# A two-layer transformer trunk in one kernel: in its linear attention, the 64-row products of the two halves of the array are issued alternately, into two PSUM banks

## The chip, the cores and the metric

The kernel runs on one core of a Trainium2 chip. The metric is device time in microseconds (us) of one execution. A profile is one further execution recorded by the hardware; its engines are PE (TensorE, the 128x128 matrix array), PEld (loads of the stationary operand into that array), DVE (VectorE), ACT (ScalarE) and SP (which issues the DMAs). GpSimd does no work here.

## The reference, cut to what matters

Two layers work on 256 latent and 256 context tokens of width 1024. Each layer projects its normalised input, feeds three token mixers (latent attention, bidirectional gated linear attention, neighbourhood attention), merges their outputs by gates, and adds a feed-forward block. Only the linear attention is touched by the change. It has 4 heads with 64-wide keys and 128-wide values, and works in chunks of 64 tokens, once forwards and once backwards:

```python
def gla_chunked(q, k, v, log_a, s0):
    ...
    cum = jnp.cumsum(log_a, axis=3)
    last = cum[:, :, :, -1:, :]
    q_dec = q * jnp.exp(cum)
    k_inv = k * jnp.exp(-cum)
    k_end = k * jnp.exp(last - cum)
    ...
    att = jnp.where(lower, jnp.einsum('bhncd,bhnsd->bhncs', q_dec, k_inv), 0.0)
    o_intra = jnp.einsum('bhncs,bhnse->bhnce', att, v)
    kv_chunk = jnp.einsum('bhncd,bhnce->bhnde', k_end, v)
    decay = jnp.exp(last[:, :, :, 0, :])
    def step(state, inp):
        dec, kv = inp
        return dec[..., None] * state + kv, state
    ...
    o_inter = jnp.einsum('bhncd,bhnde->bhnce', q_dec, s_prev)
    return (o_intra + o_inter).reshape(b, h, l, dv), s_final
```

Two of these products matter below: `kv_chunk` (sum over the 64 tokens of a chunk) and the scores `att` (sum over the 64 key channels). Both sum over 64, half of the array's 128 rows.

## The kernel before

Nothing in the kernel is issued directly. The code records every operation into a plan (`_Plan.record`), with the operations that it depends on and a price in ns (`price`). When all is recorded, `schedule` lays the operations out on a modelled clock: each engine takes the ready operation with the earliest due time, the due times follow from the prices and the recorded order of the PE operations, and a buffer is taken only when one is free. There are 8 PSUM banks of 512 fp32 columns (tag `b`), 70 general SBUF slabs (`s`), and three buffers each for raw, high and low weight tiles. `emit` then writes the instructions out in the order found; every instruction has the line of that call, L486, in the profile, so groups are told apart by tile names. On the chip each engine runs its own list in that order and waits on semaphores.

The recorded order comes from `drive`: it takes the main matrix work (`mains`, generators that yield the price of what they recorded) and, in proportion to the work done, pulls steps from a `filler` generator, up to `ftotal` in all. In the stage that matters the filler is `gla()`, the linear attention; the mains are the projections of its values (`tm` with `ev_v`, PSUM tile `zt`) and gates (`ev_g`), then `merge(1, yC)`, which alternates gate projections (`fm`, PSUM tile `z`) and output projections of the neighbourhood attention (`proj`). After it comes `merge(2, yB)`, which needs the result of the linear attention. The values that the filler yields set how fast it advances beside the mains. Weights come by DMA into `raw`, ACT rounds them to `hi`, DVE forms the rest `lo`, and three passes (hi, lo) make one product; these passes are of type float32r. The products of the linear attention are in plain float32, and each shows as two passes (two MATMUL records) in the profile.

`gla()` for one layer:

- `gla_prep`: cumulated decays by products of 64 output columns (PSUM tile `gc`), alternating between the two column halves of the array; then exponentials.
- `kv(t)`, for a tile of 128 tokens (two chunks): four transposes into `gkt`, copied by ACT into `gkT`; then for each of the two chunks (`half`) four products of 64 rows, one for each head, into a bank `gkv` of its own; DVE scales each by the decay into `gkvs` (`tensor_scalar`, four per chunk).
- `att(t)`: for each direction `d` four score products of 64 rows into a bank `gat`; DVE writes them under a mask into `attz` (`copy_predicated`), then adds both directions into `gatt`.
- `scan`: the states `gS`, by `scalar_tensor_tensor` on DVE, forwards in the upper and backwards in the lower partitions.
- `o_tile(t)`: for each head one product of 128 rows (`go<-tv,gatt`) and two of 64 output columns (`go<-gS,gqk`), for the two chunks, into the two column halves; then squares on ACT (`gjk`), a reciprocal root by small DVE steps (`grv`, `gry`, `gra`, `grb`), `gyt`, transposes `gyT`, and the split result `ybh`, `ybl`.

The first layer has 4 calls of `kv` and 4 of `att`; the second, whose context output isn't needed, 4 of `kv` and 2 of `att`. That is 14 calls, 28 runs of four products with 64 rows, 112 products, 224 passes.

The price of such a product is that of a full one, `max(4 * n / 2.4, 1.67 * m) + 5.4`, 219 for 128 columns. `record` makes one exception (L252 to L261): a float32 product with at most 64 output columns that follows one in another column half is priced at 56 (27 for 32 columns).

Of the kernel before, what the change touches and what calls it, by code (L numbers as in the profile page):

```python
# [9 lines left out]
F32 = mybir.dt.float32  # L10
# [4 lines left out]
ALU = mybir.AluOpType  # L15
# [129 lines left out]
def _meets(a, b):  # L145
    if a[1] <= b[0] or b[1] <= a[0] or a[3] <= b[2] or b[3] <= a[2]:
        return False
    if a[4] is None and b[4] is None:
        return True
    sa = a[4] if a[4] is not None else range(a[2], a[3])  # L150
    sb = b[4] if b[4] is not None else range(b[2], b[3])
    if a[4] is None:
        return any(x in sa for x in sb)
    return any(x in sb for x in sa) if b[4] is None else not sa.isdisjoint(sb)
# [27 lines left out]
class _Plan:  # L182
# [15 lines left out]
    def record(self, eng, name, args, kw):  # L198
        op = _Op()
        op.eng, op.name, op.args, op.kw, op.idx = eng, name, args, kw, len(self.ops)  # L200
        op.func = args[2] if name == "activation" else None
        w, r = [], []
        if "out" in kw:
            w.append(kw["out"])
            rest = list(args)
        else:
            w.append(args[0])
            rest = list(args[1:])
        for k, v in kw.items():
            if k == "accum_out":  # L210
                w.append(v)
            elif k != "out":
                rest.append(v)
        r = [v for v in rest if isinstance(v, _View)]
        w = [v for v in w if isinstance(v, _View)]
        if name == "copy_predicated" or (name == "matmul" and not kw.get("start", True)):
            r.append(w[0])
        deps = set()
        op.bufs = []
        op.allocs = []  # L220
        for v in r:
            g = v.region()
            deps.update(o for o, q in v.buf.writes if _meets(g, q))
        for v in w:
            g = v.region()
            if v.buf.space == "psum" and eng == "pe":
                prev = [o for o, q in v.buf.writes]
                deps.update(prev[-1:])
                deps.update(o for o, q in v.buf.reads)
            else:  # L230
                deps.update(o for o, q in v.buf.writes if _meets(g, q))
                deps.update(o for o, q in v.buf.reads if _meets(g, q))
        for v in r:
            v.buf.reads.append((op.idx, v.region()))
        for v in w:
            g = v.region()
            if v.buf.first is None:
                v.buf.first = op.idx
                op.allocs.append(v.buf)
            v.buf.writes = [x for x in v.buf.writes if not (g[4] is None and x[1][0] >= g[0] and x[1][1] <= g[1] and x[1][2] >= g[2] and x[1][3] <= g[3])]  # L240
            v.buf.reads = [x for x in v.buf.reads if not (g[4] is None and x[0] != op.idx and x[1][0] >= g[0] and x[1][1] <= g[1] and x[1][2] >= g[2] and x[1][3] <= g[3])]
            v.buf.writes.append((op.idx, g))
        for b in {id(v.buf): v.buf for v in r + w}.values():
            op.bufs.append(b)
            b.left += 1
        deps.discard(op.idx)
        op.deps = deps
        op.pin = self.last_pe if self.pinned else None
        op.cost, op.bytes = self.price(eng, name, w, r, kw)
        if eng == "pe":  # L250
            self.last_pe = op.idx
            rows = w[0].p1 - w[0].p0  # L252
            if name == "matmul" and r[0].dtype == F32 and rows <= 64:
                if self.lead and w[0].p0 not in self.lead:
                    op.cost = 56.0 if rows > 32 else 27.0
                    self.lead.add(w[0].p0)
                else:
                    self.lead = {w[0].p0}
            else:
                self.lead = set()  # L260
        self.ops.append(op)  # L261
        return op
# [227 lines left out]
def tile_trunk(ctx: ExitStack, tc: tile.TileContext, xin, wst, wm0, wmt, cbc_in, ct_in, cols_in, fin_in,  # L490
               glan_in, gw_in, nab_in, const_in, out):
    nc = _Plan(CAPS, HORIZON)

    def const_tile(shape, dt, tag, name):
        return nc.tile(tag, shape, dt, name)

    def slab(name, dt=F32, shape=None):
        return nc.tile("s", shape or [128, 512], dt, name)
# [7 lines left out]
    def bank(name, shape=None):  # L506
        return nc.tile("b", shape or [128, 512], F32, name, "psum")

    if True:
# [43 lines left out]
        gmask = (const[:, 1024:1536].bitcast(U32), const[:, 1536:2048].bitcast(U32))  # L553
        ct = const_tile([128, 8, 2], F32, "ct", "ct")
        h = []
        for k in range(KD):
            t = slab(f"x{k}")
# [3 lines left out]
        for l in range(L):  # L561
            t = const_tile([128, 69], F32, f"cols{l}", f"cols{l}")
# [365 lines left out]
        for l in range(L):  # L928
# [10 lines left out]
                                           op0=ALU.mult, op1=ALU.add)  # L939
# [206 lines left out]
            gv = [None] * 4  # L1146
            gs = [None] * 4
            qq, kk = [None] * 4, [None] * 4
# [54 lines left out]
            dec = const_tile([128, 4, 8], F32, "dec", f"dec{l}")  # L1203
# [97 lines left out]
            def gla():  # L1301
# [10 lines left out]
                bufs = []  # L1312
                for d in range(2):
                    t = slab(f"attz{d}")
# [4 lines left out]
                def kv(t):  # L1319
                    ps = bank("gkt", [128, 4, 128])  # L1320
                    for hh in range(4):
                        nc.tensor.transpose(ps[:, hh], kk[hh][:, 128 * t : 128 * t + 128], ident)
                    kt = slab("gkT")
                    nc.scalar.copy(kt, ps)
                    yield 430
                    for half in range(2):
                        r = slice(64 * half, 64 * half + 64)
                        c = 2 * t + half
                        pk = bank("gkv", [128, 4, 128])
                        for hh in range(4):  # L1330
                            nc.tensor.matmul(pk[:, hh], kt[r, 128 * hh : 128 * hh + 128], gv[t][r, 128 * hh : 128 * hh + 128], start=True, stop=True)
                        s = slab("gkvs", shape=[128, 4, 128])
                        for hh in range(4):
                            nc.vector.tensor_scalar(out=s[:, hh], in0=pk[:, hh], scalar1=dec[:, hh, c : c + 1], scalar2=None, op0=ALU.mult)
                        kvs[c] = s
                        yield 860

                def att(t):
                    w = slice(128 * t, 128 * t + 128)
                    a = slab("gatt")  # L1340
                    for d in range(2):
                        r = slice(64 * d, 64 * d + 64)
                        ps = bank("gat", [128, 4, 128])
                        for hh in range(4):
                            nc.tensor.matmul(ps[:, hh], kk[hh][r, w], qq[hh][r, w], start=True, stop=True)
                        nc.vector.copy_predicated(bufs[d], gmask[d], ps.rearrange("p a b -> p (a b)"))
                        yield 860
                    nc.vector.tensor_tensor(out=a, in0=bufs[0], in1=bufs[1], op=ALU.add)
                    atts[t] = a

# [44 lines left out]
                for cf in ([4, 5, 6, 7], [0, 1, 2, 3]):  # L1395
                    tt = (cf[0] // 2, cf[0] // 2 + 1)
                    for t in tt:
                        yield from kv(t)
                        if t in ts:
                            yield from att(t)  # L1400
                    st = scan(cf, cf[::-1], Sp, st)
                    for t in tt:
                        if t in ts:
                            o_tile(t)
                            yield 2600
                    for c in cf[1:3]:
                        del kvs[c]
                    atts.clear()
                for hh in range(4):
                    ps = bank("gyT", [128, 4, 128])  # L1410
# [20 lines left out]
            if not last:  # L1431
                h = []
                for k in range(KD):
                    t = slab(f"h{k}")
# [138 lines left out]
        for i in range(2):  # L1573
            t = slab(f"fdiag{i}")
# [5 lines left out]
        for k in range(KD):  # L1580
            c = slice(128 * (k % 4), 128 * (k % 4) + 128)
            for j in range(2):
                nc.tensor.matmul(po[j][k // 4][:, c], h[k][:, 128 * j : 128 * j + 128], fdiag[k // 4][:, c], start=True, stop=True)
        for j in range(2):
            for i in range(2):
                t = slab(f"o{j}_{i}")
# [7 lines left out]
    ps = ctx.enter_context(tc.tile_pool(name="ps", bufs=1, space=bass.MemoryType.PSUM))  # L1594
# [117 lines left out]
```

## Time and profile before

| | us |
|---|---|
| median of 3 runs | 1548.5 (1545.71 to 1548.73) |
| the profiled execution | 1543.93 |
| its span, first to last instruction | 1542.1 |
| DVE busy | 1089.3 (71%) |
| ACT busy | 763.3 (49%) |
| linear attention of layer 1, first `gkv` pass to last `gat` pass | 372.8 to 453.3 |
| the same of layer 2 | 1219.0 to 1261.9 |

The granted TensorE clock is 0.996 of full speed on average. The timeline of PE has a row for each run of equal instructions: start, length from the first start to the last end, the operation with the rows and columns of the array that it uses (64*128 is 64 rows by 128 columns), and the size of the moving operand. Passes are pipelined, so rows overlap: a pass of 256 columns lasts 0.28 us in its record but starts about 0.118 us after the one ahead of it. Costs are read from start to start.

### The profile page before, as it was taken

The page shows a single profiled execution, that of the slowest core. Times are in us where ns is not written, and L with a number is a line of the kernel's source. Part 1 is how long each engine was busy: PE and PEld are TensorE (multiplying, and loading weights), DVE is VectorE, ACT ScalarE, POOL GpSimd, SP SyncE. Part 2 cuts the span into 40 slices and gives each one's busy share as a digit, 9 for nine tenths or more (in the row PEclk, how much of TensorE's full clock was granted, in tenths as well). Part 3 has the DMA queues.
Part 4 walks back from the last instruction along what each step waited for, and adds up shares of the span by engine and source line. Part 5 has one row for each costly group of instructions (what it writes and reads, how often), then busy time and mean ns, then how long its engine had stood idle before and what let it go on. Part 6 is the DMA issues. An engine that isn't in the chain of part 4 may idle for free.

```text
span 1542.1 us, 24547 instructions
## 1 busy us (share of the span) xinstructions
PE 1523.3 (99%) x9566; PEld 1311.6 (85%) x9566; DVE 1089.3 (71%) x2174; ACT 763.3 (49%) x1363; POOL 0.2 (0%) x4
## 2 busy tenths in 40 slices
PE   8999999999999999999999999999999999999998
PEld 4687787789877899888888889887998999999998
DVE  5799989989888789633333336898476797776565
ACT  4669745576223345332232234679567535564443
POOL 0000000000000000000000000000000000000000
PEclk9999999999999999999999999999999999999999
DMA  9442244533335775622223224432342234455553
GB/s 365 148 157 99 101 157 168 172 131 123 103 110 174 248 268 179 204 93 91 92 90 100 96 91 143 143 113 82 105 145 87 99 107 164 164 195 190 178 190 112
DMA packets 67157, 222.68 MB, mean 144 GB/s; under 512 B 7964, under 2 KB 8348, under 8 KB 67040
## 3 DMA queue, kind: packets, MB, share of 16 engines
q1 hardware_dynamic: 67040, 221.11, 42.1%
q8 instruction: 75, 1.23, 0.3%
q14 instruction: 42, 0.34, 0.1%
HBM read 220.03 MB, written 1.05 MB: 143 GB/s over the span
## 4 chain that ended last, share of the span: by engine, by line
PE 94%; ACT 3%; DVE 2%; issue 0%; DMA 0%; SPq 0%; DVEq 0%
PE z L486 22%; PE fg L486 12%; PE fu L486 12%; PE fo L486 12%; PE zt L486 8%; PE proj L486 7%; PE wo L486 4%; PE zf L486 2%; PE mas L486 1%; PE nao L486 1%; PE nas L486 1%; PE mat L486 1%; PE go L486 1%; PE nat L486 1%; PE mao L486 1%; PE gkv L486 1%
## 5 line engine op out<-in xcount | busy, mean ns | idle before, releaser
L486 ACT CAST hi<-raw 128x1024 fp32r<-128x1024 f32 (+3 forms) x305 | 313.5, 1028 | 507.4 <-PE z L486 115.4
L486 DVE TENSOR_TENSOR lo<-raw,hi 128x1024 fp32r<-128x1024 f32 (+3 forms) x305 | 364.5, 1196 | 170.3 <-ACT hi L486 167.2
L486 PE MATMUL z<-uh,hi 128*128 128x512 f32 (+2 forms) x632 | 227.2, 360 | 0.0
L486 PE MATMUL z<-uh,lo 128*128 128x512 f32 (+2 forms) x632 | 219.8, 348 | 0.7 <-DVE lo L486 0.7
L486 PE MATMUL z<-ul,hi 128*128 128x512 f32 (+2 forms) x632 | 220.3, 349 | 0.0
L486 DVE SCALAR_TENSOR_TENSOR junk<-wm,cbc 128x1024 bf16<-128x1024 f32 x132 | 160.7, 1217 | 7.8 <-DMA wm<-in_wmt 6.8
L486 PEld LDWEIGHTS z<-uh,hi 128*128 128x128 f32 (+1 forms) x632 | 118.3, 187 | 23.6 <-issue 7.5
L486 PEld LDWEIGHTS z<-uh,lo 128*128 128x128 f32 (+1 forms) x632 | 118.1, 187 | 18.1 <-DVE lo L486 0.9
L486 PEld LDWEIGHTS z<-ul,hi 128*128 128x128 f32 (+1 forms) x632 | 118.4, 187 | 15.8 <-issue 0.7
L486 PE MATMUL fo<-hh,lo 128*128 128x256 f32 (+1 forms) x408 | 127.5, 314 | 0.0
L486 PE MATMUL fo<-hl,hi 128*128 128x256 f32 (+1 forms) x408 | 127.4, 314 | 0.0
L486 PE MATMUL fo<-hh,hi 128*128 128x256 f32 (+1 forms) x408 | 127.2, 314 | 0.0
L486 PE MATMUL fg<-uf,lo 128*128 128x256 f32 (+1 forms) x344 | 115.1, 335 | 0.0
L486 PE MATMUL fg<-ug,hi 128*128 128x256 f32 (+1 forms) x344 | 114.8, 334 | 0.0
L486 PE MATMUL fg<-uf,hi 128*128 128x256 f32 (+1 forms) x344 | 114.8, 334 | 0.0
L486 PE MATMUL fu<-uf,lo 128*128 128x256 f32 (+1 forms) x336 | 113.6, 338 | 0.0
L486 PE MATMUL fu<-uf,hi 128*128 128x256 f32 (+1 forms) x336 | 113.6, 338 | 0.0
L486 PE MATMUL fu<-ug,hi 128*128 128x256 f32 (+1 forms) x336 | 113.4, 338 | 0.0
L486 PE MATMUL zt<-hi,uh 128*128 128x256 f32 x352 | 102.4, 291 | 0.0
L486 PE MATMUL zt<-hi,ul 128*128 128x256 f32 x352 | 99.5, 283 | 0.0
L486 PE MATMUL zt<-lo,uh 128*128 128x256 f32 x352 | 99.1, 282 | 0.0
L486 PEld LDWEIGHTS fo<-hh,lo 128*128 128x128 f32 x408 | 76.5, 188 | 5.4
(402 smaller groups left out, 3204.8 us busy)
## 6 DMA issues: line engine op xcount, KB each, us to landing
raw<-in_wst SPq DMA_DIRECT2D x257, 512.0 KB, 3.5
wm<-in_wmt SPq DMA_DIRECT2D x82, 512.0 KB, 3.9
raw<-in_wst SPq DMA_DIRECT2D x40, 448.0 KB, 3.2
wmr<-in_wm SPq DMA_DIRECT2D x9, 512.0 KB, 7.2
nab<-in_nab SPq DMA_DIRECT2D x16, 256.0 KB, 3.8
fr<-in_wst SPq DMA_DIRECT2D x10, 256.0 KB, 5.8
raw<-in_wst SPq DMA_DIRECT2D x6, 384.0 KB, 3.0
x<-in_xin SPq DMA_DIRECT2D x8, 256.0 KB, 5.1
```

Source lines behind the costliest of these rows:

```text
L486: getattr(eng[o.eng], o.name)(*[real(a) for a in o.args], **{k: real(v) for k, v in o.kw.items()})
```

## The change

The two runs of four products in `kv(t)`, and in `att(t)`, are merged into one run of eight: two banks are taken at once, and for each head the product of the upper 64 rows is followed by that of the lower 64 rows. The DVE operations behind them are the same and in the same recorded order. The two yields of 860 become one of 1200. In `record`, the exception for the price is widened: it holds for a product with at most 64 rows too, where row half and column half together differ from those of the run so far.

```diff
             rows = w[0].p1 - w[0].p0
-            if name == "matmul" and r[0].dtype == F32 and rows <= 64:
-                if self.lead and w[0].p0 not in self.lead:
+            deep = r[0].p1 - r[0].p0
+            if name == "matmul" and r[0].dtype == F32 and min(rows, deep) <= 64:
+                at = (r[0].p0, w[0].p0)
+                if self.lead and at not in self.lead:
                     op.cost = 56.0 if rows > 32 else 27.0
-                    self.lead.add(w[0].p0)
+                    self.lead.add(at)
                 else:
-                    self.lead = {w[0].p0}
+                    self.lead = {at}
...
                     yield 430
+                    pk = [bank("gkv", [128, 4, 128]) for _ in range(2)]
+                    for hh in range(4):
+                        for half in range(2):
+                            r = slice(64 * half, 64 * half + 64)
+                            nc.tensor.matmul(pk[half][:, hh], kt[r, 128 * hh : 128 * hh + 128], gv[t][r, 128 * hh : 128 * hh + 128], start=True, stop=True)
                     for half in range(2):
-                        r = slice(64 * half, 64 * half + 64)
                         c = 2 * t + half
-                        pk = bank("gkv", [128, 4, 128])
-                        for hh in range(4):
-                            nc.tensor.matmul(pk[:, hh], kt[r, 128 * hh : 128 * hh + 128], gv[t][r, 128 * hh : 128 * hh + 128], start=True, stop=True)
                         s = slab("gkvs", shape=[128, 4, 128])
                         for hh in range(4):
-                            nc.vector.tensor_scalar(out=s[:, hh], in0=pk[:, hh], scalar1=dec[:, hh, c : c + 1], scalar2=None, op0=ALU.mult)
+                            nc.vector.tensor_scalar(out=s[:, hh], in0=pk[half][:, hh], scalar1=dec[:, hh, c : c + 1], scalar2=None, op0=ALU.mult)
                         kvs[c] = s
-                        yield 860
+                    yield 1200
...
                     a = slab("gatt")
+                    pa = [bank("gat", [128, 4, 128]) for _ in range(2)]
+                    for hh in range(4):
+                        for d in range(2):
+                            r = slice(64 * d, 64 * d + 64)
+                            nc.tensor.matmul(pa[d][:, hh], kk[hh][r, w], qq[hh][r, w], start=True, stop=True)
                     for d in range(2):
-                        r = slice(64 * d, 64 * d + 64)
-                        ps = bank("gat", [128, 4, 128])
-                        for hh in range(4):
-                            nc.tensor.matmul(ps[:, hh], kk[hh][r, w], qq[hh][r, w], start=True, stop=True)
-                        nc.vector.copy_predicated(bufs[d], gmask[d], ps.rearrange("p a b -> p (a b)"))
-                        yield 860
+                        nc.vector.copy_predicated(bufs[d], gmask[d], pa[d].rearrange("p a b -> p (a b)"))
+                    yield 1200
```

Since prices and yields set the order of the whole plan, the lists of the engines move too. Two places on PE follow; a row is one kind of product with its count.

The first is in layer 1, at the score products of one token tile. Before, the two runs of four stand with six passes of a gate projection (`z`) between them:

```order
L486 MATMUL proj<-ych,lo_4440 128x512
L486 MATMUL gat<-gqk 128x128 x4
L486 MATMUL z<-uh_0_266,hi_4443 128x512
L486 MATMUL z<-ul_0_310,hi_4443 128x512
L486 MATMUL z<-uh_0_266,lo_4458 128x512
L486 MATMUL z<-uh_1_317,hi_4443 128x512
L486 MATMUL z<-ul_1_361,hi_4443 128x512
L486 MATMUL z<-uh_1_317,lo_4458 128x512
L486 MATMUL gat<-gqk 128x128 x4
```

In the changed kernel the score products of such a tile stand between passes of a gate projection as one run:

```order
L488 MATMUL z<-ul_1_361,hi_4308 128x512
L488 MATMUL z<-uh_1_317,lo_4336 128x512
L488 MATMUL gat<-gqk 128x128 x8
L488 MATMUL z<-uh_2_383,hi_4308 128x512
L488 MATMUL z<-ul_2_392,hi_4308 128x512
```

The eight products are now one run. So it is at all 14 places: PE's list had 28 runs of four products with 64 rows, each between full products, and has 14 runs of eight.

The second place is in layer 2, at `o_tile` of the second token tile. Before, its twelve products stand together, four times one full product and the pair of the two column halves:

```order
L486 MATMUL go<-tv,gatt 128x128
L486 MATMUL go<-gS_12243,gqk 64x128
L486 MATMUL go<-gS_12190,gqk 64x128
L486 MATMUL go<-tv,gatt 128x128
L486 MATMUL go<-gS_12243,gqk 64x128
L486 MATMUL go<-gS_12190,gqk 64x128
```

In the changed kernel the beginning of the same tile reads so:

```order
L488 MATMUL go<-tv,gatt 128x128
L488 MATMUL proj<-ycl,hi_12222 128x256
L488 MATMUL go<-gS_12133,gqk 64x128
L488 MATMUL proj<-ych,lo_12297 128x256
L488 MATMUL z<-uh_0_8736,hi_12248 128x256
L488 MATMUL z<-ul_0_8909,hi_12248 128x256
L488 MATMUL proj<-ych,hi_12222 128x256
L488 MATMUL go<-gS_12061,gqk 64x128
L488 MATMUL go<-tv,gatt 128x128
L488 MATMUL go<-gS_12133,gqk 64x128
L488 MATMUL go<-gS_12061,gqk 64x128
L488 MATMUL go<-tv,gatt 128x128
```

The first pair of halves is torn apart by full products, the second still stands together. Over both tiles of layer 2 the 16 half products stood in 8 pairs, and now stand in 3 pairs and 10 single ones. In layer 1 they stay in 16 pairs.

## The prediction

> **What bounds the kernel now.** I read the page first: busy times, then the chain that ended last, then who PE waited for.
>
> ```profile
> span 1542.1 us, 24547 instructions
> PE 1523.3 (99%) x9566; PEld 1311.6 (85%) x9566; DVE 1089.3 (71%) x2174; ACT 763.3 (49%) x1363; POOL 0.2 (0%) x4
> PE 94%; ACT 3%; DVE 2%; issue 0%; DMA 0%; SPq 0%; DVEq 0%
> PE mat L486 <- DVE map L486: 3.9, 2, 2.0
> PE n0p L486 <- DVE sq L486: 1.9, 1, 1.9
> ```
>
> PE is busy for 99% of the span, and the chain that ended last runs through PE for 94% of it. The list of PE's waits begins with 3.9 us and 1.9 us, and none of its ten entries names a tile of the linear attention. So time taken out of PE's list there is time off the end, as long as nothing else comes late. A busy PE doesn't say what a product costs, though, since records overlap; that I read from start to start in PE's timeline around one run of the products.
>
> ```profile
> 372.23 0.28 PE L486 MATMUL zt<-hi,ul 128*128 128x256 f32 x1
> 372.35 0.28 PE L486 MATMUL zt<-hi,uh 128*128 128x256 f32 x1
> 372.47 0.28 PE L486 MATMUL zt<-lo,uh 128*128 128x256 f32 x1
> 372.58 0.28 PE L486 MATMUL zt<-hi,ul 128*128 128x256 f32 x1
> 372.79 1.16 PE L486 MATMUL gkv<-tv,gkT 64*128 64x128 f32 x8
> 373.88 0.39 PE L486 MATMUL zt<-hi,uh 128*128 128x256 f32 x1
> 374.10 0.28 PE L486 MATMUL zt<-lo,uh 128*128 128x256 f32 x1
> ...
> 379.38 0.28 PE L486 MATMUL zt<-hi,ul 128*128 128x256 f32 x1
> 379.59 1.16 PE L486 MATMUL gat<-gqk 64*128 64x128 f32 x8
> 380.68 0.38 PE L486 MATMUL zt<-hi,uh 128*128 128x256 f32 x1
> 380.90 0.28 PE L486 MATMUL zt<-lo,uh 128*128 128x256 f32 x1
> ```
>
> Full passes of 256 columns start every 0.118 us (372.23 to 372.58 is three of them). From 372.58 to 374.10 are 1.52 us, and two such passes lie in it, 0.24; the run of four products (8 passes) therefore costs PE **1.28 us**. The run of `gat` gives the same: 380.90 - 379.38 - 0.24 = 1.28.
>
> How that splits is in the durations of the passes, which the view of one tile lists as minimum, median and maximum.
>
> ```profile
> L486 PEld LDWEIGHTS gkv<-tv,gkT x128: 182/188/188, 372.8 to 1254.7; 64*128 64x128 f32 x128
> L486 PE MATMUL gkv<-tv,gkT x128: 272/272/374, 372.8 to 1254.8; 64*128 64x128 f32 x128
> ```
>
> The first pass of a run lasts 374 ns, the others 272: the extra 102 ns is its operand load, which nothing covers. Take 0.374 from the run's 1.16 and seven starts remain, 0.112 us a pass. So 8 x 0.112 = 0.90 is streaming, and 1.28 - 0.90 = **0.38 us is paid on entering and leaving** the 64-row form, whatever stands in the run. The next full pass (0.39 long, the one behind it 0.22 later) shows the same on the way out.
>
> **The change, part by part.** *Runs merged.* 28 runs become 14, so the 0.38 is paid 14 times less. That part is sure if the order is as built: 14 x 0.38 = 5.3 us.
>
> *Halves alternated.* No row of this trace has two row halves in turn, so the price of that is bounded by its nearest relatives. If the halves only take turns, a merged run has 16 passes of 0.112 plus 0.38, 2.17 us. If they stream side by side, two passes share a slot: 8 x 0.112 + 0.38 = 1.28, what a run of half the products costs now. The relative is the decay product `gc`, which alternates between two column halves:
>
> ```profile
> 358.36 0.28 PE L486 MATMUL zt<-hi,ul 128*128 128x256 f32 x1
> 358.57 1.09 PE L486 MATMUL gc<-const,gla 128*64 128x128 f32 x16
> 359.60 0.39 PE L486 MATMUL zt<-hi,uh 128*128 128x256 f32 x1
> 359.82 0.28 PE L486 MATMUL zt<-lo,uh 128*128 128x256 f32 x1
> ...
> L486 PEld LDWEIGHTS gc<-const,gla x128: 132/137/137, 345.9 to 1212.4; 128*64 128x64 f32 x128
> L486 PE MATMUL gc<-const,gla x128: 272/273/323, 345.9 to 1212.5; 128*64 128x128 f32 x128
> ```
>
> Its 16 passes cost 359.82 - 358.36 - 0.24 = 1.22 us: two by two they take (1.09 - 0.323) / 7 = 0.110 a slot, and the first pass shows an uncovered load of 51 ns for 64 columns, where `gkv` shows 102 for 128. Put the larger load in and the relative says 1.22 + 0.05 = 1.27, against 1.28 by the other way. I take 1.28, since it is the relative with alternation that the merged run is nearest to. Each merged run then saves 2 x 1.28 - 1.28 = 1.28, and 14 of them **17.9 us**; the other end, 2.17, leaves 14 x 0.39, about 5.4. Below 1.28 nothing is to be had, because a slot is one stream of 128 columns at 0.110 in either form.
>
> Here the Trainium skill speaks against the change. "TensorE: Matmul & The Clock Gate", section "LDWEIGHTS (loading the stationary operand)", says that a load's time goes with the columns alone, so that a load of few rows takes as long as a full one: 128 columns would be an estimated 107 ns, close to the 102 above. If the two halves' loads, 128 columns each here, then queue one behind the other, the slot of two passes is set by two loads, and the sum ends at the 5.4. "TensorEngine Tiling (Array Packing)", "Key Properties", says instead that tiles load and multiply in parallel and that only a change of mode drains the array, not a change of tile; by it the sum ends at 17.9. No run here shows row halves; the column halves agree with the second.
>
> *Pairs torn apart.* In layer 2 the order has 13 visits to the 64-column form for `go` where 8 were. What a pair and what a single one cost stands side by side once, at `gc`:
>
> ```profile
> 1198.17 0.38 PE L486 MATMUL zt<-hi,ul 128*128 128x256 f32 x1
> ...
> 1198.72 0.44 PE L486 MATMUL gc<-const,gla 128*64 128x128 f32 x4
> 1199.09 0.39 PE L486 MATMUL zt<-hi,ul 128*128 128x256 f32 x1
> 1199.41 0.43 PE L486 MATMUL gc<-const,gla 128*64 128x128 f32 x2
> 1199.77 0.39 PE L486 MATMUL zt<-hi,uh 128*128 128x256 f32 x1
> ```
>
> 1198.17 to 1199.09 is three full passes (0.35) and a pair: 0.57. 1199.09 to 1199.77 is one full pass (0.12) and a single product: 0.56. A half product alone costs as much as two, so each of the 5 visits more adds 0.56: **+2.8 us**. This one is given back whatever the rows do.
>
> *What is late next.* PE's list from the first `gkv` to the first product with `ybh` holds the same work in both kernels. In layer 2 it took 1219 to 1286; there PE becomes 6 x 1.28 - 2.8 = 4.9 us quicker, and DVE, which makes all that lies between, must follow.
>
> ```profile
> 1219.00:1287.00 68.00, 68.00 (x539) 62.72 (x539) 60.71 (x164) 26.76 (x52) 0.00 (x0) 1.00 0.34 117
> DVE lo L486 <- ACT hi L486: 3.2, 5, 1.0
> DVE grv L486 <- ACT gjk L486: 2.5, 1, 2.5
> L486 DVE TENSOR_TENSOR lo<-raw,hi 128x1024 fp32r<-128x1024 f32 x16 | 19.5, 1221 | 3.3 <-ACT hi L486 3.2
> L486 DVE SCALAR_TENSOR_TENSOR junk<-wm,cbc 128x1024 bf16<-128x1024 f32 x132 | 160.7, 1217 | 7.8 <-DMA wm<-in_wmt 6.8
> ```
>
> In this stretch DVE is busy 60.7 of 68.0 us, and 5.7 of its 7.3 idle us are waits for ACT. In the new order it has 13 weight splits `lo` between its first `gkvs` and its last `ybl` where it had 15, 2 x 1.22 = 2.4 us less. That leaves 58.3 of work and perhaps the same 5.7 of waits, 64.0, in 68.0 - 4.9 = 63.1 us: about **0.9 us** of PE waiting. The ends are 0, if those waits close up, and 4.9, if DVE ends when it does today. In layer 1 eight merged runs take 10.2 us out; DVE loses more there: ten of 18 modulation products (`junk`) and three splits `lo` stand outside the stretch now, 13 x 1.22 = 15.9 us, so I take no wait. The two banks are now taken together; PE shows no wait for a bank in these stretches, and I cost that at nothing. If a bank were late, the run would wait for DVE's four `gkvs` of the run before, part of the 4.9 above. The DMAs are the same; on SP weight and modulation loads trade places, and PE waits for no DMA in its list.
>
> **The sum**, against the profiled execution's own time of 1543.9: -17.9 + 2.8 + 0.9 = -14.2, 1529.7 us. That execution lies 4.6 us (0.3%) under the median of the runs shown, 1548.5, and 1.8 under the lowest; on the median the forecast is **1534.3 us**, 0.9% faster.
>
> **The rivals.**
>
> *The halves only take turns* (the change doesn't do what it says): 14 x 2.17 for 28 x 1.28, which is -5.4 + 2.8 + 0 (PE is hardly quicker, DVE keeps up) = -2.6, **1545.9**. For it: a load of 128 columns is as long as a pass, 188 ns in its record against 137 for 64 columns, and is hidden now only behind one stream. Against it: `gc`, whose loads run two by two as well. It is where the first of the two pages above would lead.
>
> *DVE sets the pace in layer 2*: the full 4.9 us in place of 0.9, **1538.3**. For it: 60.7 of 68.0. Against it: 2.4 us of splits leave, and PE's list has a whole gate projection between the last `gyT` and the products that need `ybh`.
>
> *Each change of half drains the array* (the other side). Entering plus leaving costs 0.38, so a drain 0.19. With 15 changes in a run of 16 passes: 15 x 0.19 = 2.9 on top of 2.17, 5.0 for 2.56, 14 x 2.5 = +35 and +2.8, **1586**. It decides from 12 ns a change: 14 x 15 x 0.012 eats the 2.6 us that are left without overlap. Against it: column halves change with no such loss (16 passes in 1.09 us). For it: rows that were never alternated here, and outputs that go to two banks at once.
>
> **How the numbers follow.** Forecast 0.70; turns only 0.15; DVE's pace 0.08; drains 0.07. About 0.2% (3.1 us) is what a measurement of this kernel can tell from no change. Forecast and DVE's pace are faster, 0.78; turns only lies just inside the bound, and I give 0.05 of it to faster, 0.09 to the same, 0.01 to slower; drains are slower. That is 0.83, 0.09, 0.08. The forecast's own range is 1528.8 (no wait, and a median as low against mine as the profiled execution was: 1534.3 - 0.9 - 4.6) to 1538.3. The range reaches up to the case of turns only and allows 0.6 us for reading its runs to 0.04 us: 1546.5; it leaves out the drains and little else.
>
> **What would show it.** Right: 14 rows of `gkv` and `gat` with x16, each about 1.16 long and 1.28 us by starts; starts in pairs a few ns apart, 0.11 from pair to pair; single `go` visits in layer 2 at 0.56. Turns only: rows of some 2.05. Drains: rows of 4 us and more, first passes longer than 272 throughout. DVE's pace: entries of PE waiting for `gS`, `gyt` or `ybl` between 1210 and 1290. I am wrong if these rows come out as forecast and the end does not follow: then something outside the linear attention has moved with the new order.

## The result, and the profile after

| | before | after |
|---|---|---|
| median, us | 1547.91 (4 runs, 1545.71 to 1548.73) | 1536.47 (4 runs, 1536.03 to 1537.5) |
| ratio | | 0.9929 [0.9912, 0.9946] |
| profiled execution, its span | 1543.93, 1542.1 | 1537.5, 1535.7 |

The changed kernel is 11.4 us (0.7%) faster; 14.2 were forecast. Of the page of the changed kernel, these lines answer to the first ones shown of before: span, busy times, and the chain that ended last.

```profile
span 1535.7 us, 24561 instructions
PE 1514.1 (99%) x9566; PEld 1301.7 (85%) x9566; DVE 1091.3 (71%) x2174; ACT 764.1 (50%) x1363; POOL 0.2 (0%) x4
PE 93%; DVE 3%; ACT 3%; issue 0%; DMA 0%; SPq 0%; DVEq 0%
```

PE still sets the time, and its busy time fell by 9.2 us. The timeline of PE in layer 1 of the changed kernel (start, length, operation, rows and columns of the array, count) shows the first merged run:

```profile
375.98 0.28 PE L488 MATMUL zt<-hi,ul 128*128 128x256 f32 x1
376.18 1.16 PE L488 MATMUL gkv<-tv,gkT 64*128 64x128 f32 x16
377.27 0.39 PE L488 MATMUL zt<-hi,uh 128*128 128x256 f32 x1
377.50 0.28 PE L488 MATMUL zt<-lo,uh 128*128 128x256 f32 x1
```

Sixteen passes in the same 1.16 us that eight took, and 377.50 - 375.98 - 0.24 = 1.28 us from start to start. All 14 runs cost 1.282 to 1.295 us that way (median 1.287).

To see where the gain stayed, I read the first start of a few tiles in both traces (each is in the view of its tile). A stage here goes from the first `gkv` of a layer to its first product with `ybh`; the same PE work lies in it in both kernels.

| us | before | after | difference |
|---|---|---|---|
| first `zf`, ahead of anything changed | 20.3 | 23.7 | +3.4 |
| stage of layer 1 | 372.79 to 496.26 = 123.47 | 376.18 to 489.40 = 113.22 | -10.25 |
| stage of layer 2 | 1219.02 to 1286.15 = 67.13 | 1212.99 to 1280.60 = 67.61 | +0.48 |

The first line is no effect of the change: PE's order there is the same, and the other profiled executions of this study, one of them of the kernel before with half of the scalings moved (below), start their first `zf` at 22.3 to 24.2. Over the first 24.8 us the granted clock is 0.93 before and 0.79 after; that this makes the whole difference is not shown. The two stages sum to -9.8, all that the two profiled executions differ by beyond that start. Layer 1 gave what was forecast (10.2). Layer 2 was to give 4.0 and gave nothing. Its waits of PE (tile, releaser: us in total, times, longest), in the trace of the changed kernel between 1205 and 1285:

```profile
PE go L488 <- DVE gS L488: 1.6, 2, 1.2
PE z L488 <- DVE lo L488: 0.7, 1, 0.7
PE gyT L488 <- ACT gt L488: 0.6, 1, 0.6
```

The third is a wait for a PSUM bank: the transposes `gyT` read nothing that ACT writes, but ACT's `gt` had first to read a `z` tile out of the bank that `gyT` takes. The kernel before had no wait of PE in this stage. The timeline of PE around the first two shows a second loss behind the waits (idle time and its releaser stand in brackets):

```profile
1242.57 0.38 PE L488 MATMUL go<-tv,gatt 128*128 128x128 f32 x2
...
1243.03 0.28 PE L488 MATMUL z<-uh,lo 128*128 128x256 f32 x1
1244.48 0.43 PE L488 MATMUL go<-gS,gqk 128*64 128x128 f32 x2 [1.17 <-DVE gS L488]
...
1245.89 0.28 PE L488 MATMUL z<-uh,lo 128*128 128x256 f32 x1
1246.64 0.53 PE L488 MATMUL go<-gS,gqk 128*64 128x128 f32 x2 [0.47 <-DVE gS L488]
...
1248.12 0.41 PE L488 MATMUL proj<-ych,lo 128*128 128x256 f32 x1
1248.33 0.41 PE L488 MATMUL proj<-ych,hi 128*128 128x256 f32 x1
1248.54 0.41 PE L488 MATMUL proj<-ycl,hi 128*128 128x256 f32 x1
```

After the second wait, full passes start every 0.21 us instead of 0.118. Busy time by stretch (PE, PEld, DVE, ACT, POOL, each with its count; granted clock of PE; DMA share; GB/s) says why:

```profile
1213.00:1280.60 67.60, 64.55 (x532) 58.55 (x531) 61.99 (x167) 26.06 (x50) 0.00 (x0) 0.97 0.35 114
1242.00:1246.60 4.60, 2.99 (x23) 2.41 (x21) 4.24 (x14) 0.51 (x1) 0.00 (x0) 1.00 0.00 0
1246.60:1250.40 3.80, 3.76 (x17) 3.44 (x17) 3.54 (x11) 0.66 (x2) 0.00 (x0) 0.55 0.00 0
```

For 3.8 us the granted clock is 0.55 (the same view gives 0.50 for 1246.85 to 1250.25 alone); that costs an estimated 3.8 x 0.45 = 1.7 us. PE idles 67.60 - 64.55 = 3.05 us in the stage, 2.3 of it for DVE and 0.6 for that bank. Together 4.8 of the 5.4 us by which the stage (67.61) exceeds PE's own list as forecast (67.13 - 7.68 + 2.8 = 62.25). The other 0.6 I can't assign.

Why does DVE come late? The first `go` stands 45.05 us behind the first `gkv` in the kernel before (1264.07 - 1219.02) and 29.58 in the changed one (1242.57 - 1212.99). Six merged runs explain 7.7 of these 15.5 us. The rest is order: 66 full passes of `z` and `proj` that stood ahead of the first `go` (186, now 120) now stand behind it, 66 x 0.118 = 7.8 us. Three of them still stand ahead of the first product with `gS`, so up to there it is 63 passes, the number that the expectation of e9 uses. Two rows of the same view, each over the 30 us after the first `gkvs`, first of the kernel before and then of the changed one:

```profile
1220.60:1250.40 29.80, 29.80 (x235) 27.98 (x233) 26.64 (x66) 11.23 (x16) 0.00 (x0) 1.00 0.36 125
```

```profile
1214.60:1244.50 29.90, 28.73 (x270) 27.24 (x269) 28.53 (x74) 11.19 (x16) 0.00 (x0) 1.00 0.38 124
```

DVE is full either way (26.64 of 29.80, 28.53 of 29.90). Before, PE asked for the first state 14 us after the end of that stretch; now it asks 1.2 us ahead of it.

### The profile page after: what moved, and what is told of

It reads as the page before. It is cut to its first block, busy times and chain, and to the rows that moved or that the text cites. A ratio compares the mean times of both kernels' runs of the same rounds, so it can differ in the third digit from the quotient of the medians.

```text
span 1535.7 us, 24561 instructions
## 1 busy us (share of the span) xinstructions
PE 1514.1 (99%) x9566; PEld 1301.7 (85%) x9566; DVE 1091.3 (71%) x2174; ACT 764.1 (50%) x1363; POOL 0.2 (0%) x4
## 3 DMA queue, kind: packets, MB, share of 16 engines
HBM read 220.03 MB, written 1.05 MB: 144 GB/s over the span
## 4 chain that ended last, share of the span: by engine, by line
PE 93%; DVE 3%; ACT 3%; issue 0%; DMA 0%; SPq 0%; DVEq 0%
PE z L488 22%; PE fo L488 12%; PE fu L488 12%; PE fg L488 12%; PE zt L488 9%; PE proj L488 6%; PE wo L488 4%; PE zf L488 2%; PE mas L488 2%; PE nao L488 1%; PE nas L488 1%; PE mat L488 1%; PE qu L488 1%; PE nat L488 1%; PE mao L488 1%; PE go L488 1%
## 5 line engine op out<-in xcount | busy, mean ns | idle before, releaser
L488 PEld LDWEIGHTS fo<-hh,hi 128*128 128x128 f32 x408 | 76.4, 188 | 5.4
```

The costliest lines, as they stand in the source:

```text
L488: getattr(eng[o.eng], o.name)(*[real(a) for a in o.args], **{k: real(v) for k, v in o.kw.items()})
```

## The experiments

Theory at the start: in layer 2 DVE sets the pace, and the torn pairs of `go` cost little beside it. Rivals: the torn pairs are worth their full 2.8 us; or layer 1 and layer 2 gained alike and something else was lost. Later two forms of the theory were told apart: LEAD (the new yields bring `go` forward to where DVE isn't ready) and TOTAL (DVE's sum of work sets the stage's length, wherever `go` stands). All kernels but one start from the changed kernel. The stage of layer 2 is from the profile, the median and ratio are against the kernel before in the same batch (1547.56, 1547.16 and 1548.22). A stage is that of one profiled execution, which need not be a middle one: e3's took 1537.35 us where its median is 1534.96, e6's 1528.55 where it is 1530.91.

| run | median | ratio [95%] | stage of layer 2 | first `gkv` to first `go` |
|---|---|---|---|---|
| changed kernel | 1536.47 | 0.9929 [0.9912, 0.9946] | 67.61 | 29.6 |
| e1 merged, halves in turn | 1540.12 | 0.9953 [0.9935, 0.9971] | 66.35 | 32.8 |
| e2 layer 1 only | 1537.55 | 0.994 [0.9926, 0.9955] | 67.09 | 45.0 |
| e3 pairs kept | 1534.96 | 0.9928 [0.9911, 0.9945] | 66.56 | 34.6 |
| e4 half the scaling on ACT | 1533.9 | 0.9916 [0.9902, 0.993] | 63.32 | 29.5 |
| e5 kernel before, same scaling | 1547.47 | 1.0 [0.9986, 1.0014] | 67.02 | 45.0 |
| e6 e3 and e4 | 1530.91 | 0.99 [0.9881, 0.992] | 60.11 | 32.9 |
| e7 e6, longer runs, 2 banks | 1525.91 | 0.9872 [0.9851, 0.9893] | 59.13 | 31.9 |
| e8 e6, longer runs, 4 banks | 1523.44 | 0.9857 [0.9832, 0.9881] | 60.61 | 31.0 |
| e9 yields of 1720 | 1534.43 | 0.9907 [0.989, 0.9925] | 63.93 | 37.3 |
| e10 e9 and pairs kept | 1529.97 | 0.9878 [0.9859, 0.9897] | 60.05 | 41.1 |
| e11 e8 with yields of 1720 | 1521.84 | 0.9831 [0.9814, 0.9848] | 58.36 | 38.7 |

### e1: what the alternation does

```diff
-                    for hh in range(4):
-                        for half in range(2):
+                    for half in range(2):
+                        for hh in range(4):
```

The same in `att`: the runs stay merged and keep their two banks, but all four upper products go ahead of the four lower ones.

> The runs of eight stay merged, in two banks, but the four products of the upper rows all come ahead of the four of the lower rows, so no two neighbours but one use different halves. If the halves stream side by side only when they alternate, and a visit to the 64-row form costs 0.38 us whatever stands in it, a run of 16 passes costs 2.17 us (0.112 a pass), layer 1 is 8 x 0.39 = 3.1 us quicker than before instead of 10.2, and the time is about 1545. If the gain came from merging alone (half the visits, or something else of the new order), the time stays at the changed kernel's, about 1536.5, and the runs at 1.28.

The timeline of PE of this kernel, at the first run:

```profile
376.05 0.28 PE L488 MATMUL zt<-hi,ul 128*128 128x256 f32 x1
376.26 1.71 PE L488 MATMUL gkv<-tv,gkT 64*128 64x128 f32 x16
377.90 0.39 PE L488 MATMUL zt<-hi,uh 128*128 128x256 f32 x1
378.12 0.29 PE L488 MATMUL zt<-lo,uh 128*128 128x256 f32 x1
```

A run costs 378.12 - 376.05 - 0.24 = 1.83 us, neither 2.17 nor 1.28. Less 0.38 this is 13 slots of 0.112 for 16 passes: three slots are shared although the order has no alternation. The single records of the run agree: at 376.814, 6 ns behind the fifth pass, one starts that is 373 ns long, as the first pass of a half is, and each half has eight, so three passes of the upper half, which stand ahead of it in PE's list, start after it. So the order matters, 1.83 against 1.28, but not as all or nothing. Layer 1 gained 8 x (2 x 1.28 - 1.83) = 5.8 by this; its stage is 5.9 shorter than before. In layer 2 the slower runs cost nothing: the stage is 1.3 us under the changed kernel's, since the first `go` stands 3.2 us later, PE waits only 0.4 us, for `gS`, and the clock stays at 1.00.

### e2: layer 1 alone

Both bodies of `kv` and `att` are kept; layer 2 takes the old one.

```diff
+                kv = kv_1 if last else kv_0
...
+                att = att_1 if last else att_0
```

> The change in layer 1 alone; layer 2 records kv and att as before. If layer 2 brought nothing (its 7.7 us of quicker runs given back to torn pairs and waits for VectorE), this kernel keeps nearly all of it: 1536 to 1538, and the stretch of layer 2 from the first gkv to the first product with ybh is 67.1 us long as before. If layer 2 did earn its 4 us and the shortfall lies elsewhere, this one is some 4 us behind the changed kernel, about 1540.5.

The median is 1.1 us over the changed kernel, and the intervals of the two ratios overlap. Layer 1's stage is 10.25 shorter, as in the changed kernel, and layer 2's 67.09, as before. The change in layer 2 brought nothing that this measurement can tell.

### e3, e4, e5, e6: pairs, DVE's load, and both

e3 gives all twelve products of `o_tile` the dependencies of the whole tile, so that the planner doesn't tear the pairs: 8 visits in layer 2 instead of 13.

```diff
                 def o_tile(t):
+                    n0 = len(nc.ops)
...
+                    both = set().union(*[o.deps for o in nc.ops[n0:]])
+                    for o in nc.ops[n0:]:
+                        o.deps |= {d for d in both if d < n0}
```

> As the changed kernel, but in o_tile every product depends on all that the twelve products of the tile wait for, so the order keeps the pairs of column halves together (8 visits in layer 2 instead of 13). If torn pairs are what ate layer 2's gain, their 2.8 us come back: about 1533.7, and the stretch of layer 2 is 64.8 us. If VectorE sets the pace there, the time that PE gains turns into waiting: 1536 to 1537, stretch about 67 us, with PE waits for gS or for products behind it.

e4 leaves the order of the change nearly as it is (13 visits, the first `go` behind the same 120 full passes) and moves 16 of layer 2's 32 scalings of `gkvs` (and as many of layer 1's) from DVE to ACT; e5 does the same to the kernel before.

```diff
-                            nc.vector.tensor_scalar(out=s[:, hh], in0=pk[half][:, hh], scalar1=dec[:, hh, c : c + 1], scalar2=None, op0=ALU.mult)
+                            if hh % 2:
+                                nc.scalar.activation(s[:, hh], pk[half][:, hh], AF.Copy, scale=dec[:, hh, c : c + 1])
+                            else:
+                                nc.vector.tensor_scalar(out=s[:, hh], in0=pk[half][:, hh], scalar1=dec[:, hh, c : c + 1], scalar2=None, op0=ALU.mult)
```

> As the changed kernel, but every second of the scalings gkvs (half the heads) is done by ScalarE instead of VectorE; 16 of 32 leave VectorE in layer 2, 16 x 0.344 = 5.5 us. The pairs stay torn. If VectorE sets the pace in layer 2, the PE waits there (3.6 us from start to start) shrink and the time comes to about 1533; if torn pairs and not waits are the loss, it stays at 1536.5 and the stretch of layer 2 at 67.6 us.

> The kernel before, with every second of the scalings gkvs on ScalarE as in e4; nothing else. If the relief of VectorE helps only where PE has become too quick for it, it is worth nothing here: 1547 to 1548, stretch of layer 2 67.1 us. If the move to ScalarE is a gain of its own (a shorter chain whatever PE does), it shows here too: about 1544.5.

> e3 and e4 together: pairs kept, half of the scalings on ScalarE. If VectorE was what took back the kept pairs' gain in e3, they now show: up to 2.8 us under e4, 1531 to 1532, stretch of layer 2 60.5 to 61.5 us. If VectorE still sets the pace, it stays at e4's 1533.9 and 63.3 us.

PE's waits of e3 between 1205 and 1285, and its stretch behind the longest:

```profile
PE go L488 <- DVE gatt L488: 1.6, 1, 1.6
PE go L488 <- DVE gS L488: 0.9, 1, 0.9
PE gyT L488 <- ACT gt L488: 0.6, 1, 0.6
PE z L488 <- DVE lo L488: 0.2, 1, 0.2
```

```profile
1246.00:1250.00 4.00, 1.49 (x11) 0.89 (x9) 3.94 (x13) 0.80 (x1) 0.00 (x0) 1.00 0.00 0
1250.00:1254.00 4.00, 4.00 (x21) 2.50 (x20) 3.97 (x7) 0.50 (x3) 0.00 (x0) 0.51 0.31 90
1254.00:1268.00 14.00, 14.00 (x106) 12.83 (x106) 9.95 (x39) 6.26 (x19) 0.00 (x0) 0.90 0.29 92
```

Five visits fewer took 2.8 us from PE's list, and 1.05 came off the stage: PE waits 2.5 us at one place, and the clock is down to 0.51 and 0.90 behind it. In e4, one of these entries is left:

```profile
PE go L488 <- DVE gS L488: 0.6, 1, 0.6
```

The stage is 4.3 us shorter. The control e5 says that the move itself is worth nothing: ratio 1.0 where PE didn't wait. So the 4.3 are waits and what hangs on them: PE's idle time in the stage fell from 3.05 to 0.65 us, and the 1.7 of lowered clock are gone. With both (e6) no wait is left, and the pairs are worth 63.32 - 60.11 = 3.2 us, 0.65 of them e4's last wait, where they were worth 1.05 with DVE late. Taken one by one, the two edits give 1.05 + 4.3; together they give 7.5.

### e9, e10: where DVE's lateness comes from

The changed kernel also lowered the values that the filler yields, from 860 + 860 to 1200 for each merged step. e9 puts their sum back and leaves all else; e10 also keeps the pairs.

```diff
-                    yield 1200
+                    yield 1720
```

> The changed kernel, but the merged steps yield 1720 (twice 860, the old sum) instead of 1200. In layer 2 the list then has 301 rows of PE between the first gkv and the first go, as before the change, where the changed kernel has 238; the 14 merged runs and the 13 visits for go stay. Theory LEAD (the wait for gS in the changed kernel is there because the smaller yields put go 63 full passes, 7.4 us, earlier on PE's list, on top of the 7.7 us that the runs lose): the waits go, the stage of layer 2 from the first gkv to the first product with ybh is 67.1 - 7.7 + 2.8 = 62.3 to 62.9 us with the clock at 1.00, and the median about 5 us under the changed kernel, 1531 to 1532. Theory TOTAL (DVE's sum of work over the whole stage, 62 us and 5 to 6 of waiting, sets its length, wherever go stands): the waits only move to a later place, the stage stays at 66 to 67.6 us and the median at 1535 to 1537.

> As the run with the old yields, and the pairs of go kept together (8 visits in layer 2); the first go stands 333 rows behind the first gkv. LEAD: stage of layer 2 59.5 to 60.2 us, median 1528.5 to 1529.5, without any scaling moved to ACT. TOTAL: stage not under 64, since DVE's list is the same; median not under 1533.

In e9 the first `go` stands 37.33 us behind the first `gkv`: the 45.05 of before less the 7.7 of six merged runs. The stage shrank by 3.7 us to 63.93, and PE's waits in it are these two, the second for a bank; neither brought the clock down:

```profile
PE go L488 <- DVE gS L488: 0.7, 1, 0.7
PE z L488 <- ACT gt L488: 0.5, 1, 0.5
```

```profile
1213.30:1277.20 63.90, 62.72 (x531) 56.94 (x531) 59.61 (x160) 26.38 (x50) 0.00 (x0) 1.00 0.36 119
```

That lies between the two forecasts, nearer to LEAD's (62.3 to 62.9) than to TOTAL's (66 to 67.6). Its median does not tell them apart: 1534.43 lies between LEAD's 1531 to 1532 and TOTAL's 1535 to 1537, nearer to TOTAL's. e10 decides: DVE has no less to do (15 splits `lo` between its first `gkvs` and its last `ybl`, as before the change, where the changed kernel has 13), and its stage is 60.05 with no wait of PE; its median, 1529.97, is 0.5 over LEAD's range and 3 under TOTAL's.

```profile
1212.60:1272.60 60.00, 59.82 (x531) 55.66 (x531) 57.57 (x160) 26.43 (x50) 0.00 (x0) 1.00 0.39 124
```

TOTAL had said not under 64. So DVE's sum of work does not set the stage; the order does. That it is the distance between the products that feed the states and the products that read them is read from the waits, which name `gS`; the yields move DVE's list too, and no run moved `go` alone.

### e7, e8, e11: fewer and longer runs

The entry cost invites still longer runs. e7 puts the `kv` and `att` products of a tile in one run, and in `o_tile` groups the column halves of two heads, in two banks; e8 takes a bank for each head; e11 is e8 with yields of 1720. All three contain e6.

```diff
+                    if t in ts:
+                        pas[t] = att_products(t)
                     for half in range(2):
                         c = 2 * t + half
...
-                    po = bank("go", [128, 4, 128])
-                    for hh in range(4):
-                        nc.tensor.matmul(po[:, hh], atts[t][:, 128 * hh : 128 * hh + 128], gv[t][:, 128 * hh : 128 * hh + 128], start=True, stop=False)
-                        for half in range(2):
+                    pb = [bank("go", [128, 4, 128]) for _ in range(4)]
+                    po = [pb[hh % 4][:, hh] for hh in range(4)]
+                    for h0 in range(0, 4, 4):
+                        for hh in range(h0, h0 + 4):
+                            nc.tensor.matmul(po[hh], atts[t][:, 128 * hh : 128 * hh + 128], gv[t][:, 128 * hh : 128 * hh + 128], start=True, stop=False)
+                        for hh in range(h0, h0 + 4):
+                            for half in range(2):
```

> e6, and three kinds of visits merged further: the products of kv and att of one token tile in one run (16 products, 4 banks; 8 runs instead of 14), and in o_tile the column-half products of two heads in one run (2 banks; 12 visits instead of 24). If a visit costs what it did (0.38 us for 64 rows, 0.35 for 64 columns), that is 6 x 0.38 + 12 x 0.35 = 6.5 us under e6, about 1525; if VectorE paces layer 2, only the part in layer 1 (4 x 0.38 + 8 x 0.35 = 4.3 us) is left, 1527 to 1528.

> As e7, with one bank for each head in o_tile, so all eight column-half products of a tile can be one run; the order has 9 visits instead of 12. By the visits 1 us under e7; if eight banks are too few for four at once, PE waits for banks and it is slower than e7.

> The version with the longest runs (scaling half on ACT, kv and att in one run of 16 products, one bank for each head in o_tile), with yields of 1720. It has 1.6 us of PE waiting for DVE in layer 2 with 1200. LEAD: these go, the median is 1.5 to 3 us under it, 1520.5 to 1522. TOTAL: no gain, 1523 to 1524.

The timeline of PE of e8 at the first such run:

```profile
375.10 0.28 PE L488 MATMUL zt<-hi,ul 128*128 128x256 f32 x1
375.31 1.16 PE L488 MATMUL gkv<-tv,gkT 64*128 64x128 f32 x16
376.30 1.06 PE L488 MATMUL gat<-gqk 64*128 64x128 f32 x16
377.29 0.39 PE L488 MATMUL zt<-hi,uh 128*128 128x256 f32 x1
377.52 0.28 PE L488 MATMUL zt<-lo,uh 128*128 128x256 f32 x1
```

377.52 - 375.10 - 0.24 = 2.18 us for both, where two runs of 1.28 are 2.56: one entry of 0.38 less. e7 came out 5.0 us under e6, where 6.5 or 4.3 was expected. e8 is 2.5 under e7, where 1 was expected, but that four banks are better than two is not shown: the intervals of the ratios overlap, and in the profiles e8's two stages are 0.5 us longer together (107.86 + 60.61 against 108.86 + 59.13). One of its waits in layer 2, 0.6 us of `go` for `gyt`, is for a bank, since `go` doesn't read `gyt`. e7's profile lost time elsewhere, at 1033.1 and 1323.2, where its clock was 0.50 for 3.4 us each; e8's has no such place between 31 and 1515. e11, 1.6 under e8, has the lowest median: 26.4 us, 1.7%, under the kernel before; its ratio's interval overlaps e8's. Its profile still has one wait in layer 2, 0.9 us of `go` for `gyt`, again for a bank, which the old yields didn't take away.

## Why the prediction was right, and where its sum was off

**Right: the sign, and the merged, alternated runs.** A run cost 1.287 us where 1.28 was forecast, in pairs of starts 6 ns apart and 0.112 from pair to pair. The first passes of the two halves are 374 and 373 ns long in the records: the uncovered loads lie side by side, they don't queue. Here the Trainium skill, "TensorEngine Tiling (Array Packing)", section "Key Properties", which has tiles load and multiply in parallel, agrees with the trace; the queue of loads that the prediction weighed against it does not show. Where nothing else came late, nearly all of the 17.9 us is there: e10 is 18.3 us faster than before, and its two stages lost 10.24 and 7.08, 17.3 together.

**Right: layer 1 without a wait**, -10.25 for 10.2. No merged run waits for a bank, there or in layer 2; the one wait for a bank, 0.6 us at `gyT` in layer 2, stands far behind them, and the forecast had no term for it.

**Right in size, hidden in part: the torn pairs.** They cost 2.8 in PE's list: e9 without its 1.2 us of waits, less e10, is 63.93 - 1.2 - 60.05 = 2.7. Where PE waits for DVE later anyway (e3), keeping them brings 1.05.

**Mis-sized: PE's waiting in layer 2**, forecast at 0.9 with ends of 0 and 4.9 and put down to DVE, measured at 4.8 (3.05 idle, of which 2.3 for DVE, and 1.7 of lowered clock). The signature is that of the rival "DVE sets the pace", whose time was 1538.3; the median 1536.5 lies between it and the forecast. But the step that failed is neither's sum. The forecast gave DVE 64.0 us from the first `gkv` to the last `ybl`, and it took 63.9 (1212.99 to 1276.9), 58.3 of it busy, as summed. What I did not look at is when PE asks first. I compared two totals over a stage, as if PE could wait for DVE only at its end; the change had also lowered the yields, `go` came 7.8 us forward on top of the 7.7, and PE asked in the middle, where DVE works without a break. With the first `go` set back (e9, e10) the wait goes, in part or whole. With less for DVE to do ahead of it (e4, e6) it goes as well.

**Missed: that a wait costs more than its length.** The clock behind it was no term of the sum. The Trainium skill, "TensorE: Matmul & The Clock Gate", section "What's actually happening", puts the half clock behind an idle window of some 3.4 us. Here gaps of 1.17 and 0.47 us within 3.6 us were enough, so the measurement differs, and decides; that the clock then stays low for about such a window agrees (0.50 for 3.4 us).

Idle time alone doesn't decide it either. In the kernel before, a wait of 2.04 us leaves the clock at 1.00, and one of 0.67 us is followed by 0.50:

```profile
1045.58 0.63 PE L486 MATMUL mat<-const,map 128*128 128x128 f32 x4 [2.04 <-DVE map L486]
1341.08 1.05 PE L486 MATMUL n2l1p<-zc,n2sq 128*128 128x1 f32 x8 [0.67 <-DVE n2sq L486]
```

```profile
1045.40:1048.80 3.40, 3.22 (x18) 2.63 (x19) 3.01 (x7) 3.33 (x7) 0.00 (x0) 1.00 0.19 39
1342.40:1345.70 3.30, 3.30 (x16) 3.30 (x17) 2.95 (x15) 1.70 (x3) 0.00 (x0) 0.50 0.49 158
```

The same wait of 0.67 us in the changed kernel, ahead of 1335.55, lowered nothing. So the 1.7 us can't be forecast from the length of a wait; what decides stays open.

**Off without consequence: the price of the drains.** The list alternates by product, and a product is two passes, so a run has 7 changes of half, not 15: 7 x 0.19 = 1.3 on top of 2.17 is 3.5 for 2.56, +13 in 14 runs in place of +35. No such loss shows in the runs.

Open: the last 0.4 to 0.7 us by which each stage of layer 2 exceeds PE's list, and how much of e9's remaining waits is still lead: 0.7 us names `gS`, the other 0.5 is for a bank. That the lowered clock costs its 1.7 us is worked out from the granted clock, not tried by itself.

## What to carry to other kernels

Small products that use half of the array cost their entry into that form, so put more of them in one run (e7 is 5.0 us under e6) and alternate the halves product by product; where a run takes so many banks that the next one waits for them, as in e8, the gain is no longer sure. When an edit also changes a planner's prices or yields, look up in the new order how far each consumer stands behind its producer, and compare that distance, not the stage's totals, with what the slower engine must do in between. A version that moves a consumer forward and one that relieves its producer look alike in the waits; undo the first before paying for the second.

## What the runs showed of the hardware that was not expected

- Products of one row half start ahead of products of the other half that stand before them in PE's list: without any alternation (e1), three of 16 slots were shared, 1.83 us for a run instead of 2.17.
- A lowered clock can follow short waits: 1.64 us idle within 3.6 us gave 0.50 for 3.4 us. The length of the wait does not decide: 0.67 us gave 0.50 once and nothing another time, 2.04 us gave nothing (kernel before and changed kernel), and the waits of 0.5 to 0.7 us in the stage of e4 and e9 gave nothing.
- A run costs 0.38 us once, and 0.112 a slot, whether the slot holds one pass (8 in 1.28 us), two (16 in 1.287) or the run goes over four banks (32 in 2.18).
